# The order of weight casts and PSUM copies on ScalarE, and the places of four operand tiles, in a decoder step

## The chip, the cores and the metric

The kernel runs on one core of a Trainium2 chip. A core has TensorE (PE in the profile; PEld is its weight load), VectorE (DVE), ScalarE (ACT), GpSimd (POOL) and SyncE (SP), which here issues the DMA transfers. Each engine works through its own queue of instructions in order; semaphores tie the engines together. The metric is the device time of one execution in microseconds. Matmul operands are read from SBUF, results are summed in PSUM and must be copied or added out of it before a bank is used anew.

## The reference

One layer of a hybrid decoder runs for 1024 prompt positions and 64 sample positions (8 sequences of 8), all in float32, with a model width of 1024 and an inner width of 2816:

```
h = rmsnorm(x, norm_mix)
q, k, v, gu, gv, ga, gb = split_in(h @ w_in)
o = sink_attention(q, k, v)                      # branch A, window of 128
s = gelu(gu) * spatial_gating(layernorm(gelu(gv)))   # branch B, chunks of 128
x = x + (sigmoid(ga) * (o @ w_pa) + sigmoid(gb) * (s @ w_pb)) @ w_out
z = rmsnorm(x, norm_ffn) @ w_up                  # 1024 -> 2 * 2816
c = causal depthwise conv of width 3 over z
a, b = split(c)
x = x + (gelu(a) * b) @ w_down
y = rmsnorm(x, norm_final)
```

The outputs are y for both groups, the new key, value and convolution states and the normalised gMLP rows.

## The kernel before

Float32 products are made from matmuls in a rounded 32-bit format. `split(hi, lo, src)` (L41) makes the two parts of an operand: ScalarE casts `hi` from `src`, then VectorE subtracts to get `lo`. A product is then three matmuls, hi by hi, hi by lo, lo by hi. For weights the two parts are called `wh` and `wl`.

Two blocks of 128 weight columns are taken together as a pair, and the pair's 2 by 2 block product is done with seven products in place of eight (Winograd's form). For this the weights need four sums (`ws`, made on VectorE by `Weights.total`, L178) beside three raw blocks (`wraw`, loaded from HBM), seven units in all, each with its own cast and subtraction. The positions are cut into two groups: group 0 has half-rows of 288 columns, group 1 of 256. The left and right operands of group 0 lie in four tiles `t`, one for each quarter kk of the contraction, with the seven combinations and both parts (planes) in one tile; those of group 1 lie in `th` and `tl`. `both_planes` allocates the former, in a pool for the branch-A pairs and in another for the up pairs.

`Chain.product(j, w)` does one of the seven products for one group: four quarters by three matmuls, twelve in all (L310). Products 0, 2, 4 and 6 sum in bank `a`, and others in banks `d` and `c`, so a later product on a bank waits until the earlier state of it has been copied out. `keep` (L289 a copy, L291 a copy with a factor of −1) brings bank contents to SBUF on ScalarE as `k`; VectorE adds a bank to a kept copy (L296); L336 copies the last result out on ScalarE into `zb`.

`Weights.get(ahead, loads)` hands out the weights of the next unit and emits, at that point of the program, the load, sum, cast and subtraction of units up to `ahead` further on; the pairs ask for 3 ahead. The program's order is only a preference: a scheduler fills each engine's queue from its estimate of when things are ready. So casts may stand in ScalarE's queue far ahead of the place where they were emitted, and between copies.

The stages, in us of the profiled execution: up to 90 the v and gv projections (L528), from 90 to 460 the branch-A pairs (q, k, gu, gates; L310), from 460 to 770 attention, the gMLP, the merge and w_out (L242 and others), from 770 to 810 the operands of the FFN, from 810 to 1270 the up pairs (L310 again), and from 1270 the down projection (L1679) and the final norm.

In the up stage 22 pairs are done (f = 0 to 21, z for a and b halves in `za` and `zb`). Three of them, f = 0, 1, 2, run for group 0 alone at the start; their group-1 half follows at places 6, 13 and 21 of the list `order`. There PE does seven products of one group only ("single pair"), against fourteen in the others. After each pair, `finish(f)` does the convolution and the gate: on ScalarE a first term (L1557) and two gelu (L1608, L1611), on VectorE two terms for each half (L1558, L1559), the gate's products (L1613, L1614), and with every second pair four sums (L1621 to L1624) of what the down stage reads, which are stored to `td` in HBM.

Of the kernel before, what the change touches and what calls it, by code (L numbers as in the profile page):

```python
# [6 lines left out]
F32 = mybir.dt.float32  # L7
F32R = mybir.dt.float32r
I32 = mybir.dt.int32
AF = mybir.ActivationFunctionType  # L10
# [5 lines left out]
P = 128  # L16
# [18 lines left out]
def layer(tc, a):  # L35
    nc = tc.nc
    V, S, G, PE = nc.vector, nc.scalar, nc.gpsimd, nc.tensor

    def split(hi, lo, src, pin=False):

        for x in (S.copy(hi, src), V.tensor_sub(lo, src, hi.bitcast(F32))):  # L41
            if pin:
                tc.keep_in_program_order(x)

    def scale_split(hi, lo, src, by):
        S.activation(hi, src, AF.Copy, scale=by)
        V.scalar_tensor_tensor(lo, src, by, hi.bitcast(F32), ALU.mult, ALU.subtract)

    with ExitStack() as top:
# [22 lines left out]
        class Weights:  # L72
# [109 lines left out]
            def emit(self, upto):  # L182
                while self.emitted < min(upto, len(self.units)):
                    i, j = self.units[self.emitted]
                    _, k, dest = self.items[i]
                    if j not in ("own", "pre") and dest and not dest[0]():
                        break
                    self.load(i + 1)
                    t = self.raw[i][0] if j != "pre" else None
                    if j == "pre":  # L190
                        h, l = self.slot() if k > 4 else self.half(True)
                        for e, to in enumerate((h, l)):
                            self.last = nc.sync.dma_start(to[:, 0:k].bitcast(F32), dest[:, e])
                    elif j == "own":
                        h, l = self.half(False)
                        split(h, l, dest(t))
                    elif j == "dest":
                        h, l, hd, ld = dest[1]()
                        split(hd, ld, by256(t))
                    elif j == "full":  # L200
                        self.left = None
                        h, l = self.slot()
                        split(h[:, 0:k], l[:, 0:k], t[:, 0:k, :])
                    else:
                        h, l = self.half(j != "half")
                        src = t[:, 0:k, :]
                        if j != "half":
                            tb = self.raw[i][1]
                            src = (lambda: t[:, 0:4], lambda: self.total("s1"),
                                   lambda: self.total("s2"), lambda: self.total("s4"),  # L210
                                   lambda: self.total("s3"), lambda: t[:, 4:8],
                                   lambda: tb[:, 4:8])[j]()
                        split(h, l, src)
                    self.made[self.emitted] = (h, l)
                    self.emitted += 1
                    if self.emitted == len(self.units) or self.units[self.emitted][0] != i:
                        self.raw.pop(i)
                        self.sums = {}
# [13 lines left out]
        def by256(t):  # L232
            return t.rearrange("p (k h) c -> p k (h c)", h=2)
# [16 lines left out]
        def line(pool, n):  # L250

            pool.tile([P, n // 4], F32, name=f"gap{next(gaps)}", bufs=1)

        tx = [{}, {}]
# [4 lines left out]
        def right(stack, name, bufs=1):  # L259
            return stack.enter_context(tc.tile_pool(name=name, bufs=bufs, side="right", reuse_waits="tile"))  # L260

        def both_planes(pool, name):
            t = pool.tile([P, 7, 2, 288], F32R, name=name)
            line(pool, 64)
            return t[:, :, 0], t[:, :, 1]

        def combine(t4, b11, b12, b21, b22, eng=G):
# [9 lines left out]
        class Chain:  # L277
# [7 lines left out]

            def keep(self, name, src, by=1.0):
                t = self.keeps.tile([P, 288], F32, name="k" + name, bufs=2)[:, :self.n2]
                if by == 1.0:
                    S.copy(t, src)  # L289
                else:  # L290
                    S.activation(t, src, AF.Copy, scale=by)  # L291
                self.kept[name] = t

            def put(self, e, half, op, x, y):
# [3 lines left out]
            def product(self, j, w):  # L298
                name = ("adbadbc" if self.spread else "adadaca")[j]
                if self.spread:  # L300
                    j = SPREAD[j]
                first = name not in self.bank
                if first:
                    self.bank[name] = self.ps.tile([P, 512], F32, name="st")[:, :self.n2]
                ps = self.bank[name]
                wh, wl = w
                for kk in range(4):
                    th, tl = (x[:, (0, 1, 2, 6, 3, 5, 4)[j]] for x in self.tx[kk])
                    for i, (u, v) in enumerate(((wh, th), (wh, tl), (wl, th))):
                        PE.matmul(ps, u[:, kk, :], v, start=first and kk + i == 0,  # L310
                                  stop=kk == 3 and i == 2, skip_group_check=True)
                kept = self.kept
                if j == 0:
                    self.keep("1", ps)
                elif j == 1:
                    self.keep("5", ps)
                elif j == 2:
                    self.keep("u", ps)
                    if self.spread:
                        G.tensor_sub(kept["n"], kept["n"], kept["u"])  # L320
                        self.put(1, 1, G.tensor_sub, kept["n"], kept["5"])
                elif j == 3:
                    self.put(0, 1, V.tensor_add, kept["u"], ps)
                elif j == 4:
                    self.keep("n", ps, -1.0)
                    if not self.spread:
                        self.put(1, 1, G.tensor_sub, kept["n"], kept["5"])
                elif j == 5:
                    self.put(0, 0, V.tensor_add, kept["1"], ps)
                elif self.spread:  # L330
                    for to, lo, hi in self.places(1, 0):
                        V.scalar_tensor_tensor(to, pick(ps, to, lo, hi), -1.0, pick(kept["u"], to, lo, hi),
                                               ALU.mult, ALU.subtract)
                else:
                    for to, lo, hi in self.places(1, 0):
                        S.activation(to, pick(ps, to, lo, hi), AF.Copy, scale=-1.0)  # L336

        def pick(x, place, lo, hi):
            x = x[:, lo:hi]
            return x.rearrange("p (b t) -> p b t", t=8) if len(place.shape) == 3 else x  # L340
# [35 lines left out]
        with ExitStack() as ph1:  # L376
# [58 lines left out]
            order = [*range(FEW, 9), 0, *range(9, 15), 1, *range(15, NFF), 2]  # L435
# [203 lines left out]
            t0h, xr = right(th0, "T0h"), right(xro, "xr")  # L639
            txa = [{}, {}]  # L640
# [20 lines left out]
            def t0_job(kk):  # L661
                def go():
                    first, t4, rest = sums_of(0, kk)
                    txa[0][kk] = th, tl = both_planes(t0h, f"t{kk}")
                    split(th[:, 0], tl[:, 0], first)
                    split(th[:, 1:5], tl[:, 1:5], t4)
                    split(th[:, 5:7], tl[:, 5:7], rest)
                return go
# [317 lines left out]
            def acc2():  # L986
                return pmm.tile([P, 1024], F32, name="mm")
# [284 lines left out]
            for go in merge(0, 0, keep):  # L1272
                go()
            attention(groups[1], [x for c in range(1, KD) for x in merge(0, c, keep)])
            kvo.close()
            bo[0].close()
# [56 lines left out]
            for c in range(KD):  # L1333
                for at, go in enumerate(merge(1, c, operand(1))):
                    if at == 1:
                        t, u = held.pop(c)
# [37 lines left out]
            for c in range(KD):  # L1374
                xt = x_next(0, c)
                w, ps = W.get(), acc2()
# [9 lines left out]
            t0p = right(t0o, "T0")  # L1386
# [38 lines left out]
            def t0_split(kk):  # L1425

                def go():
                    x0, x1, t4 = hx.pop(kk)
                    tx[0][kk] = th, tl = both_planes(t0p, f"t0{kk}")
                    split(th[:, 0], tl[:, 0], x0[:, 0:288])  # L1430
                    split(th[:, 5:7], tl[:, 5:7], x1.rearrange("p (h c) -> p h c", h=2))
                    split(th[:, 1:5], tl[:, 1:5], t4)
                return go
# [3 lines left out]
            for c in range(KD):  # L1437
                xt = x_next(1, c)
                w, ps = W.get(1 if c < 7 else 4), acc2()
# [492 lines left out]
```

## Time and profile before

| | us |
|---|---|
| runs | 1510.43, 1511.06, 1516.56 |
| median | 1511.06 |
| profiled execution | 1511.13 |
| its span | 1509.4 |
| PE busy | 1493.9 |
| DVE busy | 1175.3 |
| ACT busy | 851.9 |
| POOL busy | 267.9 |

The span is the time from the first to the last recorded instruction, and the profiled execution's time is 1.7 us longer. Busy times are shares of the span in which an engine worked on at least one instruction; matmuls overlap in the pipeline, so a matmul's duration (0.28 to 0.3 us) is longer than the distance from its start to the next one's (0.11 to 0.13 us). In rows of a timeline the columns are the start, the duration, the engine, the line, the operation, the tiles written and read, the form and a count; square brackets give idle time ahead and who ended it. A row with x2 stands for two instructions that overlap.

### The profile page before, as it was taken

To read this page: it belongs to the slowest core of one execution; us is meant where nothing else is said; L and a number is where in the kernel's file an instruction comes from. 1 tells how busy PE (TensorE), PEld (TensorE's weight loads), DVE (VectorE), ACT (ScalarE), POOL (GpSimd) and SP (SyncE) were. 2 spreads that over 40 slices of the span, in tenths; PEclk is the share of its full clock that TensorE was granted. 3 is DMA by queue.
4 is the path that set the end of the run, shared out by engine and by line. 5 is a ranking of instruction groups with operands and counts; after the bars stand their busy time and mean duration, and the time that the engine had idled before them with its cause. 6 is when DMAs were issued, how large, how long until landed. Compare 5 with 4: busy or idle time off the path is not lost.

```text
span 1509.4 us, 30138 instructions
## 1 busy us (share of the span) xinstructions
PE 1493.9 (99%) x11538; PEld 1454.6 (96%) x11538; DVE 1175.3 (78%) x1892; ACT 851.9 (56%) x1778; POOL 267.9 (18%) x381
## 2 busy tenths in 40 slices
PE   9999999999999999999999999999999999999998
PEld 9999999999998989998989999999999999999998
DVE  7798877755576877979667988898899888685686
ACT  8557676654455765864453555555555556353463
POOL 0001000010030222320134422332142222000002
PEclk9999999999999999999999999999999999999999
DMA  7688446864779757438988323332232216983463
GB/s 257 220 275 273 153 164 223 254 211 143 244 234 291 217 178 233 159 130 303 334 297 289 134 107 122 116 124 108 101 133 109 102 65 236 328 288 103 113 186 126
DMA packets 134431, 289.88 MB, mean 192 GB/s; under 512 B 15760, under 2 KB 36560, under 8 KB 134288
## 3 DMA queue, kind: packets, MB, share of 16 engines
q1 hardware_dynamic: 134144, 287.96, 56.9%
q8 instruction: 90, 1.47, 0.4%
q14 instruction: 53, 0.43, 0.1%
q10 hardware_dynamic: 144, 0.01, 0.0%
HBM read 198.97 MB, written 90.92 MB: 192 GB/s over the span
## 4 chain that ended last, share of the span: by engine, by line
PE 81%; DVE 6%; ACT 4%; DMA 4%; issue 3%; POOL 1%; SPq 0%; POOLq 0%; ACTq 0%; DVEq 0%
PE st L310 43%; PE dn L1679 13%; PE mm L242 13%; PE st L528 7%; PE po L1226 2%; PE sc L1175 2%; DVE wl L41 1%; DMA stg<-sd 1%; PE pt L1202 1%; DMA v<-gvd 1%; ACT wh L41 1%; PE mx L809 1%; ACT s L1192 1%; DMA kd<-q 0%; DMA stg<-vnd 0%
## 5 line engine op out<-in xcount | busy, mean ns | idle before, releaser
L310 PE MATMUL st<-t,wh 128*128 128x288 f32 x2128 | 428.6, 294 | 3.0 <-ACT k L289 1.6
L310 PEld LDWEIGHTS st<-t,wh 128*128 128x128 f32 x2128 | 335.9, 188 | 4.0 <-ACT k L289 2.2
L310 PE MATMUL st<-t,wl 128*128 128x288 f32 x1064 | 312.5, 294 | 0.0
L310 PE MATMUL st<-th,wh 128*128 128x256 f32 x1064 | 295.5, 278 | 1.9 <-ACT k L289 1.8
L310 PE MATMUL st<-tl,wh 128*128 128x256 f32 x1064 | 294.2, 277 | 0.0
L310 PE MATMUL st<-th,wl 128*128 128x256 f32 x1064 | 293.9, 276 | 0.0
L310 PEld LDWEIGHTS st<-th,wh 128*128 128x128 f32 x1064 | 199.8, 188 | 3.3 <-ACT k L289 2.9
L310 PEld LDWEIGHTS st<-th,wl 128*128 128x128 f32 x1064 | 199.9, 188 | 0.0
L310 PEld LDWEIGHTS st<-t,wl 128*128 128x128 f32 x1064 | 199.8, 188 | 0.0
L310 PEld LDWEIGHTS st<-tl,wh 128*128 128x128 f32 x1064 | 199.7, 188 | 0.0
L1679 PE MATMUL dn<-th,wh 128*128 128x288 f32 (+1 forms) x616 | 176.9, 287 | 0.8 <-ACT zb L336 0.6
L1679 PE MATMUL dn<-tl,wh 128*128 128x288 f32 (+1 forms) x616 | 176.2, 286 | 0.0
L1679 PE MATMUL dn<-th,wl 128*128 128x288 f32 (+1 forms) x616 | 175.2, 284 | 0.2 <-DVE wl L41 0.2
L41 ACT CAST wh<-wraw 128x512 fp32r<-128x512 f32 (+2 forms) x188 | 129.5, 701 | 81.2 <-DMA wraw<-wt 34.2
L41 DVE TENSOR_TENSOR wl<-wraw,wh 128x512 fp32r<-128x512 f32 (+2 forms) x188 | 148.6, 804 | 30.3 <-ACT wh L41 28.2
L41 ACT CAST wh<-ws 128x512 fp32r<-128x512 f32 x168 | 102.6, 621 | 95.4 <-PE st L310 58.1
L41 DVE TENSOR_TENSOR wl<-ws,wh 128x512 fp32r<-128x512 f32 x168 | 119.1, 719 | 44.3 <-ACT wh L41 43.4
L1679 PEld LDWEIGHTS dn<-th,wh 128*128 128x128 f32 x616 | 115.6, 188 | 1.3 <-ACT zb L336 0.9
L1679 PEld LDWEIGHTS dn<-th,wl 128*128 128x128 f32 x616 | 115.9, 188 | 0.4 <-DVE wl L41 0.4
L1679 PEld LDWEIGHTS dn<-tl,wh 128*128 128x128 f32 x616 | 115.7, 188 | 0.0
L528 PE MATMUL st<-w2h,hh 128*128 128x256 f32 x288 | 80.5, 280 | 0.4 <-ACT rst L494 0.4
L528 PE MATMUL st<-w2l,hh 128*128 128x256 f32 x288 | 80.0, 278 | 0.0
(277 smaller groups left out, 3165.1 us busy)
## 6 DMA issues: line engine op xcount, KB each, us to landing
wraw<-wt SPq DMA_DIRECT2D x137, 512.0 KB
traw<-td SPq DMA_DIRECT2D x77, 272.0 KB
td<-za SPq DMA_DIRECT2D x22, 544.0 KB
q<-qd SPq DMA_DIRECT2D x16, 512.0 KB
upd<-hl SPq DMA_DIRECT2D x14, 512.0 KB
td<-t SPq DMA_DIRECT2D x11, 544.0 KB
wpart<-wt SPq DMA_DIRECT2D x22, 256.0 KB
qd<-q SPq DMA_DIRECT2D x8, 576.0 KB
```

Source lines behind the costliest of these rows:

```text
L41: for x in (S.copy(hi, src), V.tensor_sub(lo, src, hi.bitcast(F32))):
L242: PE.matmul(ps[:, lo:lo + c1 - c0], u[:, k, :], v[:, c0:c1], start=(k == 0 and i == 0), stop=(k == nk - 1 and i == 2))
L310: PE.matmul(ps, u[:, kk, :], v, start=first and kk + i == 0, stop=kk == 3 and i == 2, skip_group_check=True)
L528: PE.matmul(ps, u[:, lo:lo + P], v[:, k, :], start=k + i == 0, stop=k == KD - 1 and i == 2)
L809: PE.matmul(ps[:, P * i:P * i + P], vn[:, i], late["wst"][:, c, :], start=True, stop=True)
L1175: PE.matmul(ps[:, h, o0:256], q, kst[kv][:, e, k0:cur + P], start=e == 0, stop=e == 1)
L1192: S.activation(s[:, h], s[:, h], AF.Exp, bias=nm[:, h:h + 1], accum_out=dn[:, h:h + 1])
L1202: PE.transpose(pt[:, h * P:h * P + P], s[:, h, 0:P], ident)
L1226: PE.matmul(po, v[:, kv, :], t, start=e == 0, stop=last)
L1679: PE.matmul(place(m, e), u[:, m, :], v[:, lo:hi], start=new and i + k == 0 and (e == 0 or m % 2 == 0), stop=i == NU - 1 and k == 2, skip_g ...
```

## The change

Two things change. First, a list `row` and a function `in_row` are added: each instruction given to it depends, without a semaphore, on the last one given to it, so the scheduler has to keep them in the program's order on ScalarE's queue. Given to it are the casts of pair weights (and no other casts), the copies in `keep`, and the copies of the last product (L336). All other ScalarE instructions, such as the convolution, may still stand anywhere between them.

Second, `both_planes` is called with the quarter kk, and allocates all four tiles `t` at the first call, in the order 2, 0, 1, 3, with rows of 64 bytes between them (ahead of 2, 0 and 3, and behind 3; none between 0 and 1). Before, each tile was followed by 64 bytes. A tile has 7 · 2 · 288 · 4 = 16128 bytes, 63 times 256.

```diff
+    row = []
+
+    def in_row(x):
+
+        if row:
+            tc.add_manual_dep(x.ins, row[-1].ins.name,
+                              mybir.DependencyInfo(mybir.DependencyClass.NoSync, mybir.DependencyReason.DATA),
+                              reason="in_row")
+        row[:] = [x]
...
+    def split(hi, lo, src, pin=False, order=None):
+
+        for n, x in enumerate((S.copy(hi, src), V.tensor_sub(lo, src, hi.bitcast(F32)))):
             if pin:
                 tc.keep_in_program_order(x)
+            if order and n == 0:
+                order(x)
...
-                        split(h, l, src)
+                        split(h, l, src, order=in_row)
...
-        def both_planes(pool, name):
-            t = pool.tile([P, 7, 2, 288], F32R, name=name)
-            line(pool, 64)
+        planes = {}
+
+        def both_planes(pool, name, kk):
+            if kk == 0:
+                for x, gap in ((2, 64), (0, 64), (1, 0), (3, 64)):
+                    if gap:
+                        line(pool, gap)
+                    planes[x] = pool.tile([P, 7, 2, 288], F32R, name=f"{name}{x}")
+                line(pool, 64)
+            t = planes.pop(kk)
             return t[:, :, 0], t[:, :, 1]
...
-                if by == 1.0:
-                    S.copy(t, src)
-                else:
-                    S.activation(t, src, AF.Copy, scale=by)
+                in_row(S.copy(t, src) if by == 1.0 else S.activation(t, src, AF.Copy, scale=by))
...
-                        S.activation(to, pick(ps, to, lo, hi), AF.Copy, scale=-1.0)
+                        in_row(S.activation(to, pick(ps, to, lo, hi), AF.Copy, scale=-1.0))
...
-                    txa[0][kk] = th, tl = both_planes(t0h, f"t{kk}")
+                    txa[0][kk] = th, tl = both_planes(t0h, "t", kk)
...
-                    tx[0][kk] = th, tl = both_planes(t0p, f"t0{kk}")
+                    tx[0][kk] = th, tl = both_planes(t0p, "t0", kk)
```

Lines of the changed kernel lie some 16 lower: L310 becomes L326, L289 and L291 both become L307, L336 becomes L352, L41 becomes L51, L178 becomes L190, L1557 to L1559 become L1573 to L1575, L1679 becomes L1695.

More of the change, by code (lines that the diff above doesn't have):

```diff
@@ L37, in layer @@
     V, S, G, PE = nc.vector, nc.scalar, nc.gpsimd, nc.tensor
-    def split(hi, lo, src, pin=False):
-        for x in (S.copy(hi, src), V.tensor_sub(lo, src, hi.bitcast(F32))):
+    row = []
[7 more added lines that the diff above has]
+        for n, x in enumerate((S.copy(hi, src), V.tensor_sub(lo, src, hi.bitcast(F32)))):
             if pin:
                 tc.keep_in_program_order(x)
+            if order and n == 0:
+                order(x)
     def scale_split(hi, lo, src, by):
```

## The prediction

> **What bounds the kernel now.** I read the top of the page first, then the chain of waits, the costly groups, and last the stretches and single rows of the two stages that the change touches. The span, the busy times and two of the 40-slice rows:
>
> ```profile
> span 1509.4 us, 30138 instructions
> PE 1493.9 (99%) x11538; PEld 1454.6 (96%) x11538; DVE 1175.3 (78%) x1892; ACT 851.9 (56%) x1778; POOL 267.9 (18%) x381
> ...
> PE   9999999999999999999999999999999999999998
> ...
> PEclk9999999999999999999999999999999999999999
> ...
> PE 81%; DVE 6%; ACT 4%; DMA 4%; issue 3%; POOL 1%; SPq 0%; POOLq 0%; ACTq 0%; DVEq 0%
> ...
> L310 PE MATMUL st<-t,wh 128*128 128x288 f32 x2128 | 428.6, 294 | 3.0 <-ACT k L289 1.6
> ```
>
> TensorE is busy for 99% of the span at full clock and holds 81% of the chain that ended last. No work on PE is removed, so the time can fall by two things only: PE's idle time, and the distance between the starts of its matmuls. The waits of PE (us in total, times, longest) say how little idle time the ordered instructions cause:
>
> ```profile
> PE st L310 <- ACT k L289: 3.4, 4, 1.5
> PE st L310 <- ACT kn L291: 1.3, 1, 1.3
> ...
> PE dn L1679 <- ACT zb L336: 0.6, 1, 0.6
> ```
>
> That is 4.7 us in the pair products and 0.6 at the start of the down stage, 5.3 in all. It is the ceiling of what a better order on ScalarE can give. What a worse one can cost has no such ceiling, so I look at the slack. Stretches of the branch-A pairs, of the up pairs, and of 24 us around the first pair whose products run for group 1 alone ("single pair" below); columns are the length, then each engine's busy time:
>
> ```profile
> 90.00:460.00 370.00, 365.47 (x2989) 363.67 (x2988) 265.45 (x436) 217.56 (x434) 46.19 (x58) 1.00 0.66 218
> 810.00:1270.00 460.00, 459.02 (x3735) 457.86 (x3735) 399.34 (x579) 258.49 (x514) 134.77 (x192) 1.00 0.35 128
> 966.00:978.00 12.00, 12.00 (x104) 11.86 (x103) 11.41 (x15) 8.61 (x17) 2.85 (x2) 1.00 0.38 135
> 978.00:990.00 12.00, 12.00 (x101) 12.00 (x100) 12.00 (x16) 7.92 (x15) 7.34 (x8) 1.00 0.31 123
> ```
>
> In the branch-A pairs DVE is 72% busy (265.45 of 370) and 4.5 us of PE time are lost, some of it to the waits above. In the up pairs PE loses 1.0 us, DVE is 87% busy, and around a single pair it is full: 23.4 of 24 us. There only weights made ahead of use keep PE fed. ACT is at most 72% busy (8.61 of 12), so the order on it costs nothing by its own load; it costs where an ACT instruction waits and others stand behind it.
>
> **The change, part by part.** Counts of instructions stay the same on every engine. In program order, 920 of ACT's some 1540 instructions change place, 986 on DVE, 284 on SP's queue, 43 on POOL, 97 on PE. The casts move back by 3 to 13 places: each now sits between the copies where the program asks for it, three units ahead of its use, while before they ran as far ahead as buffers allowed. SP's moved loads of weights free their raw tile later by as much; over 810 to 1270 the DMA share is 0.35, so I cost them at nothing, and in R3 with the rest.
>
> *Placement.* A T tile is 16128 bytes, 63 times 256, so the one row of 64 bytes between tiles puts them 64 apart modulo 256: in the built program t0 to t3 lie at 224, 32, 96 and 160 before, and at 96, 96, 32 and 160 after. The starts of one product of group 0, twelve matmuls, three to a tile:
>
> ```profile
> 984.34 0.42 PE L310 MATMUL st<-t,wh 128*128 128x288 f32 x2
> ...
> 984.73 0.42 PE L310 MATMUL st<-t,wh 128*128 128x288 f32 x2
> ...
> 985.12 0.43 PE L310 MATMUL st<-t,wh 128*128 128x288 f32 x2
> ...
> 985.52 0.42 PE L310 MATMUL st<-t,wh 128*128 128x288 f32 x2
> ...
> 985.91 0.28 PE L310 MATMUL st<-th,wh 128*128 128x256 f32 x1
> ```
>
> The four tiles take 0.39, 0.39, 0.40 and 0.39 us here: 1.57 for twelve. Means of the same starts over all 266 such products (2128 + 1064 matmuls, 12 each) are 393.5 ns for the tile at 224, 392.5 at 32, 398.9 at 96, 393.0 at 160, together 1577.9. If a tile's own place sets its time, after gives 398.9 + 398.9 + 392.5 + 393.0 = 1583.3, +5.4 ns, times 266 = +1.4 us. If the step from one place to the next sets it (steps between 128 and 134 ns in these starts, some pairs of places not seen), I get 1576.5 to 1582.5, −0.4 to +1.2 us. Ends: four tiles at the best triple, −2.1; four at the worst, +4.7. I take +0.7, between the two readings. The Trainium skill ("TensorE: Matmul & The Clock Gate", section "Wait — 56ns, not 53.3ns?") gives a warm start-to-start of N/2.4 GHz plus about 2.5 ns, with no word of an operand's address; by it placement is worth nothing and the sum would be 0.7 lower. The rows disagree in size: for N = 288 it gives 122.5 ns, and twelve steps here are 1.57 us, 131 each; the measurement decides.
>
> *The order on ACT, place (i): third product of a single pair.* It accumulates on the first product's bank, so it waits for the copy k. Around the second single pair, ACT and PE:
>
> ```profile
> 1102.55 0.38 ACT L336 ACTIVATE zb<-st 128x256 f32<-128x256 f32 x1
> 1102.82 0.61 ACT L41 CAST wh<-wraw 128x512 fp32r<-128x512 f32 x1
> 1103.34 1.31 ACT L1557 ACTIVATE c<-zb,cw 128x1104 f32<-128x1104 f32 x1
> 1104.55 1.06 ACT L1608 ACTIVATE za<-c 128x1024 f32<-128x1024 f32 x1
> 1105.50 0.25 ACT L1611 ACTIVATE za<-c 128x64 f32<-128x64 f32 x1
> 1105.64 0.63 ACT L289 COPY k<-st 128x256 f32<-128x256 f32 x2
> ```
> ```profile
> 1102.28 0.28 PE L310 MATMUL st<-th,wh 128*128 128x256 f32 x1
> ...
> 1105.67 0.76 PE L310 MATMUL st<-th,wh 128*128 128x256 f32 x2
> ...
> 1260.02 0.38 PE L310 MATMUL st<-th,wh 128*128 128x256 f32 x1 [0.24 <-ACT k L289]
> ```
> ```profile
> 1106.06 150.23 PE st L310 x1225
> ```
>
> The single pair's first product starts at 1102.28 and the copy lets PE go on at 1106.06: 3.78 us. The pair's two products last 24 steps of 0.1137 (the mean of all group-1 steps; 30 steps from 1102.28 to 1105.67) = 2.73, so 1.05 is open. Before, ten matmuls of a following product were moved ahead and 0.27 was left (1106.06 − 1105.67 − 0.11); in the changed program's order they are behind, and the same six ACT instructions (zb, cast, c, the two gelu, k) stand in a row there. Three places, 1.0 each, against 0, 0.27 and, at the third (1260.02), 0.24 before: **+2.5**. Were the conv work not in the way, the waits of before would go, −0.5.
>
> *Place (ii): the pair after a single pair.* In the new order its copies k of the second product stand behind a cast of a sum, and the sum stands on DVE behind the conv of the single pair. First place, ACT then DVE:
>
> ```profile
> 985.12 0.65 ACT L289 COPY k<-st 128x288 f32<-128x288 f32 x2
> 985.89 0.62 ACT L41 CAST wh<-ws 128x512 fp32r<-128x512 f32 x1
> ```
> ```profile
> 978.18 0.41 DVE L296 TENSOR_TENSOR za<-k,st 128x256 f32<-128x256 f32 x1
> ...
> 980.73 1.36 DVE L1558 SCALAR_TENSOR_TENSOR c<-za,cw,c 128x1104 f32<-128x1104 f32 x1
> 982.01 0.68 DVE L41 TENSOR_TENSOR wl<-ws,wh 128x512 fp32r<-128x512 f32 x1
> 982.62 1.35 DVE L1559 SCALAR_TENSOR_TENSOR c<-za,cw,c 128x1104 f32<-128x1104 f32 x1
> 983.89 1.36 DVE L1558 SCALAR_TENSOR_TENSOR c<-zb,cw,c 128x1104 f32<-128x1104 f32 x1
> 985.17 0.68 DVE L178 TENSOR_TENSOR ws<-wraw 128x512 f32<-128x512 f32 x1
> ```
>
> Before, k came ahead of the cast (985.12 against 985.89) and nothing stalled. After: ACT's c 1.31, DVE's four c by 1.28 and three wl and ws by 0.61 (both from start to start) = 6.95, the cast 0.62, the copy 0.38: 9.26 us. From the end of the single pair's sixth product, PE has its seventh, 1.37, and three products of both groups at 1.58 + 1.37 = 2.94 each: 10.2. That would be 0.9 us of slack, but DVE reaches the conv 2.55 us late (978.18 to 980.73). Late by 9.26 + 2.55 − 10.2 = 1.6, and with some 0.1 for each of five handovers 2.1; the first product's copy, behind c of zb, adds an estimated 0.5. Lower end 0 (DVE takes the sums first), upper end 2.9. I take 2.6 at this place, 0.7 at the second, where fewer early units were missing, none at the third, after which the down stage starts: **+3.3**. If these stalls go, DVE's wl is late next.
>
> *Smaller costs.* The wl behind these casts come late in the single pairs (+0.6, two waits of some 0.3, between 0 and 1.5). The down stage's first wait, 0.6, grows by 0.3, as one more cast stands ahead of zb. In the branch-A pairs one wl stands behind DVE's evacuations, +0.5 (0 to 1).
>
> *Relief in the branch-A pairs.* The longest wait for kn comes behind two casts:
>
> ```profile
> 306.56 1.12 ACT L41 CAST wh<-ws 128x512 fp32r<-128x512 f32 x2
> ```
>
> In the new order both come after kn: 1.1 of the 1.3 goes. Of the four waits for k the longest, 1.5, stays (the cast there is replaced by another), and two of the other three, 1.9 together, lose a cast of about half a microsecond each: −1.3. Together **−2.4**.
>
> Sum: 0.7 + 2.5 + 3.3 + 0.6 + 0.3 + 0.5 − 2.4 = **+5.5 us**. The profiled execution took 1511.13 us (span 1509.4), 0.07 over the median of the runs, so 1511.1 + 5.5 = 1516.6.
>
> **The rivals.** *R1, faster:* the new order takes away stalls and makes none. For it: ACT is idle for 44% of the span, the waits it removes are in the trace, and three units are some 9 us of matmuls ahead (3 × 2.94). Against it: DVE full around the single pairs. It decides if DVE reaches the conv less than 0.4 us late (10.2 − 9.26 − 0.5) at place (ii) and ACT has done the gelu before k at (i). Time: −2.4 to −5.3, placement −0.4 to −2.1: 1503.7 to 1508.3, middle 1506. *R2, nothing PE sees:* the buffers of weights cover both the relief and the stalls; for it stands that PE loses only 1.0 us in 460 now. Time: 1511 plus placement 0 to +1.4: 1511 to 1512.5. *R3, overload carries on:* the late casts free raw tiles late, loads land late, and the stalls of (i) and (ii) come back in the following pairs, where DVE at 87% needs long to catch up. The 7.2 of costs double: 1511.1 + 14.4 − 2.4 + 0.7 = 1523.8. Against it: DMA share 0.35, and 13% free on DVE win back 2.5 us in one pair of 20.6 us.
>
> **How the numbers follow.** Forecast, 1513 to 1519.5: 0.50. R1 0.16, R2 0.14, R3 0.20 (1519.5 to 1525). Leaving out 0.2 at both ends together, the range is 1507 to 1522. A measurement here tells 0.5%, 7.6 us, from no change: below 1503.5 lies about a third of R1, 0.05; above 1518.6 R3 and a few hundredths of the forecast, 0.23; the rest is 0.72.
>
> **What would show it.** Right: waits of PE for k in the three single pairs of about 1 us, one of 2 us or more in the pair after the first; the 1.3 for kn gone; tile triples at 96 near 399 ns. Wrong: the placement if a product of group 0 takes less than 1.572 us or more than 1.59; place (ii) if PE's up stage loses under 3 us in all; the relief if PE's waits in the branch-A pairs stay above 3 us; the whole, if new waits stand where no conv runs.

## The result, and the profile after

The changed kernel takes 1528.7 us (median of six runs, 1526.0 to 1531.7) against 1511.1 before: a ratio of 1.0106, with a 95% interval of 1.0085 to 1.0128. By the medians it is 17.6 us slower, by the ratio 16.0. Forecast were 5.5 us more and a range up to 1522. The profiled execution is the shortest of the six, 1526.0, with a span of 1524.3, which is 14.9 more than the span before; the other runs lie up to 5.7 us higher, two of them with a mean granted TensorE clock of 0.995 and 0.996 in place of the 0.998 of the profiled one (3 to 5 us over such a span).

The page of the changed kernel and the waits of PE (us in total, times, longest):

```profile
span 1524.3 us, 30018 instructions
...
PE 76%; DVE 10%; DMA 5%; ACT 4%; issue 3%; POOL 1%; SPq 0%; POOLq 0%; ACTq 0%; DVEq 0%
...
L326 PE MATMUL st<-t,wh 128*128 128x288 f32 x2128 | 429.2, 295 | 5.0 <-ACT k L307 4.9
```
```profile
PE st L326 <- ACT k L307: 10.2, 10, 2.0
PE dn L1695 <- ACT zb L352: 1.7, 1, 1.7
PE pt L1132 <- DVE s L1125: 1.3, 1, 1.3
...
PE st L326 <- DVE wl L51: 1.1, 3, 0.6
```

PE holds 76% of the chain that ended last in place of 81%, and DVE 10% in place of 6%. PE's waits for copies `k` rose from 3.4 to 10.2 us, and by the page's rows the idle time ahead of the pair products' matmuls with `t` and `wh` from 3.0 to 5.0, with `th` and `wh` from 1.9 to 5.3; the wait of 1.3 for `kn` is gone, as forecast. By the first and last matmul of each stage, in us:

| stretch | before | after | difference | forecast |
|---|---|---|---|---|
| up to the first pair product | 109.9 | 110.6 | +0.7 | 0 |
| branch-A pairs | 349.0 | 352.6 | +3.6 | −1.9 |
| from there to the up pairs | 351.2 | 352.6 | +1.4 | 0 |
| up pairs | 456.3 | 464.4 | +8.1 | +6.4 |
| down projection to the end | 243.1 | 244.2 | +1.1 | +0.3 |

(The +0.7 for places is left out of the column of the forecast; it was not split by stage.) In the up pairs the forecast was nearly right, and in the branch-A pairs it had the wrong sign. The difference there is the least certain: in the other profiled kernels whose casts and copies stand as before in that stage, it took 345.2 to 349.1 us, and in those with the row bound 350.6 to 358.6. Of the +1.4 behind them, 0.8 is the wait of the first transposes for `s` (1.3 above, 0.5 before). The place that I had worked out in most detail, the pair behind the first single pair, in the changed kernel's rows of ACT, DVE and PE:

```profile
993.46 0.65 ACT L307 COPY k<-st 128x288 f32<-128x288 f32 x2
...
998.13 0.62 ACT L51 CAST wh<-ws 128x512 fp32r<-128x512 f32 x1 [2.56 <-DVE ws L190]
998.66 0.67 ACT L307 COPY k<-st 128x288 f32<-128x288 f32 x2
```
```profile
994.25 1.36 DVE L1574 SCALAR_TENSOR_TENSOR c<-zb,cw,c 128x1104 f32<-128x1104 f32 x1
...
996.14 1.36 DVE L1575 SCALAR_TENSOR_TENSOR c<-zb,cw,c 128x1104 f32<-128x1104 f32 x1
997.42 0.69 DVE L190 TENSOR_TENSOR ws<-wraw 128x512 f32<-128x512 f32 x1
```
```profile
999.10 0.40 PE L326 MATMUL st<-t,wh 128*128 128x288 f32 x1 [1.97 <-ACT k L307]
```

ACT stands idle for 2.56 us before a cast whose sum DVE reaches only behind the conv; the two copies stand behind that cast, and PE waits 1.97 us for the first of them. The copy is that of the pair's second product, whose last matmul for group 0 had started at 991.93, so the result had lain in PSUM for some 6 us.

### The profile page after: what moved, and what is told of

Its sections match the earlier page's. It is cut to its first block, busy times and chain, and to the rows that moved or that the text cites. A ratio compares the mean times of both kernels' runs of the same rounds, so it can differ in the third digit from the quotient of the medians.

```text
span 1524.3 us, 30018 instructions
## 1 busy us (share of the span) xinstructions
PE 1498.7 (98%) x11538; PEld 1454.6 (95%) x11538; DVE 1158.0 (76%) x1892; ACT 851.4 (56%) x1778; POOL 302.8 (20%) x381
## 4 chain that ended last, share of the span: by engine, by line
PE 76%; DVE 10%; DMA 5%; ACT 4%; issue 3%; POOL 1%; SPq 0%; POOLq 0%; ACTq 0%; DVEq 0%
PE st L326 38%; PE dn L1695 13%; PE mm L254 13%; PE st L544 6%; DVE wl L51 2%; PE po L1242 2%; DMA v<-gvd 2%; PE sc L1191 1%; DVE tl L51 1%; PE pt L1218 1%; DVE c L1574 1%; DVE c L1575 1%; DMA stg<-sd 1%; ACT wh L51 1%; PE mx L825 1%
## 5 line engine op out<-in xcount | busy, mean ns | idle before, releaser
L326 PE MATMUL st<-t,wh 128*128 128x288 f32 x2128 | 429.2, 295 | 5.0 <-ACT k L307 4.9
L326 PEld LDWEIGHTS st<-t,wh 128*128 128x128 f32 x2128 | 335.6, 188 | 6.9 <-ACT k L307 6.5
L326 PE MATMUL st<-t,wl 128*128 128x288 f32 x1064 | 313.2, 294 | 1.4 <-DVE wl L51 1.1
L326 PE MATMUL st<-th,wh 128*128 128x256 f32 x1064 | 296.0, 278 | 5.3 <-ACT k L307 5.3
L326 PE MATMUL st<-th,wl 128*128 128x256 f32 x1064 | 295.2, 277 | 0.3
L326 PE MATMUL st<-tl,wh 128*128 128x256 f32 x1064 | 294.8, 277 | 0.0
L326 PEld LDWEIGHTS st<-th,wh 128*128 128x128 f32 x1064 | 200.0, 188 | 6.5 <-ACT k L307 6.5
L326 PEld LDWEIGHTS st<-t,wl 128*128 128x128 f32 x1064 | 200.1, 188 | 3.6 <-DVE wl L51 3.4
L326 PEld LDWEIGHTS st<-th,wl 128*128 128x128 f32 x1064 | 199.9, 188 | 1.3 <-DVE wl L51 1.3
L326 PEld LDWEIGHTS st<-tl,wh 128*128 128x128 f32 x1064 | 199.8, 188 | 0.0
L51 DVE TENSOR_TENSOR wl<-ws,wh 128x512 fp32r<-128x512 f32 x168 | 120.6, 732 | 103.4 <-ACT wh L51 102.8
L1695 PE MATMUL dn<-th,wh 128*128 128x288 f32 (+1 forms) x616 | 177.2, 288 | 1.9 <-ACT zb L352 1.7
L1695 PE MATMUL dn<-tl,wh 128*128 128x288 f32 (+1 forms) x616 | 176.5, 287 | 0.0
L51 DVE TENSOR_TENSOR wl<-wraw,wh 128x512 fp32r<-128x512 f32 (+2 forms) x188 | 149.9, 808 | 34.7 <-ACT wh L51 33.6
L1695 PE MATMUL dn<-th,wl 128*128 128x288 f32 (+1 forms) x616 | 175.6, 285 | 0.2 <-DVE wl L51 0.2
L51 ACT CAST wh<-wraw 128x512 fp32r<-128x512 f32 (+2 forms) x188 | 128.8, 706 | 53.1 <-DMA wraw<-wt 31.7
L1695 PEld LDWEIGHTS dn<-th,wh 128*128 128x128 f32 x616 | 115.8, 188 | 2.3 <-ACT zb L352 1.9
L1695 PEld LDWEIGHTS dn<-th,wl 128*128 128x128 f32 x616 | 116.0, 188 | 0.4 <-DVE wl L51 0.4
L1695 PEld LDWEIGHTS dn<-tl,wh 128*128 128x128 f32 x616 | 115.8, 188 | 0.0
L51 ACT CAST wh<-ws 128x512 fp32r<-128x512 f32 x168 | 100.4, 619 | 25.2 <-DVE ws L190 25.0
L307 ACT ACTIVATE kn<-st 128x256 f32<-128x256 f32 (+1 forms) x76 | 30.0, 397 | 125.8 <-PE st L326 125.8
L1586 POOL COPY zb<-stc 128x18 f32<-128x18 f32 x22 | 65.6, 2983 | 108.5 <-DVE c L1575 92.4
```

What stands on the lines that cost most here:

```text
L51: for n, x in enumerate((S.copy(hi, src), V.tensor_sub(lo, src, hi.bitcast(F32)))):
L307: in_row(S.copy(t, src) if by == 1.0 else S.activation(t, src, AF.Copy, scale=by))
L326: PE.matmul(ps, u[:, kk, :], v, start=first and kk + i == 0, stop=kk == 3 and i == 2, skip_group_check=True)
L1586: G.tensor_copy(z[:, 0:90].rearrange("p (b t) -> p b t", t=10)[:, :, 0:2], stc[:, f + e * NFF])
L1695: PE.matmul(place(m, e), u[:, m, :], v[:, lo:hi], start=new and i + k == 0 and (e == 0 or m % 2 == 0), stop=i == NU - 1 and k == 2, skip_g ...
```

## The experiments

Unless a diff says otherwise, an experiment is an edit of the changed kernel. Ratios are to runs of the kernel before on the same chip. "Stage lengths" are taken as in the table above, from the profiled execution.

**The order alone, the places alone.** In the first the old `both_planes` is put back; in the second the three calls of `in_row` are taken out. All instructions stand on every engine as in the changed kernel in the first, as in the kernel before in the second.

```diff
-                for x, gap in ((2, 64), (0, 64), (1, 0), (3, 64)):
-                    if gap:
-                        line(pool, gap)
+                for x in range(4):
                     planes[x] = pool.tile([P, 7, 2, 288], F32R, name=f"{name}{x}")
-                line(pool, 64)
+                    line(pool, 64)
```

> The order of ScalarE's casts and copies is bound as in the changed kernel, the four T tiles stay at their old places. Theory O (the order costs nearly all): 15 to 18 us over the kernel before, the same stalls of TensorE as in the changed kernel (about 2 us in the pair after the first single pair, 1.1 us in each single pair, 1.9 us near 301 us), and a clean product of group 0 back at 1578 ns. Theory P (the uneven places cost it): within 3 us of the kernel before.

> The four T tiles lie at the new places, the order of all instructions on every engine is that of the kernel before. Theory O: within 1.5 us of the kernel before, a clean product of group 0 at 1576 ns against 1578, which is 0.6 us less over 266 products. Theory P: 12 us or more over the kernel before.

Measured: the order alone 1529.8 us, ratio 1.0115 (1.0097 to 1.0132), PE's waits for `k` 9.8 us. The places alone 1509.2, ratio 0.9986 (0.9974 to 0.9997), 2.1 us under the kernel before. The order costs all of it, and the new places give about 2 us. Of these 2, a product of group 0 explains 0.5 (1578 to 1576 ns, times 266); the rest is not tied to a place. This kernel is the fastest of all that were run.

**The order in one half only.** With the old places, a switch binds the row up to the up pairs, or from there on.

```diff
-        if row:
+        if not row_on[0]:
+            row.clear()
+            return
+        if row:
...
+        row_on[0] = False      # True in the other
         rest = []
         for f in range(FEW):
```

> Old places; the order is bound only up to the end of the merge, so in the branch-A pairs alone. If the profiles' split by stage holds: branch-A pairs 3.6 us longer, the stretch behind them 1.5 us longer, up pairs unchanged, together 4 to 6 us over the kernel before. By my prediction's relief of 2.4 us: 1 to 2 us under it.

> Old places; the order is bound only from the up pairs on. If the profiles' split by stage holds: up pairs 8 us longer, start of the down stage 1 us later, together 8 to 10 us over the kernel before, branch-A pairs unchanged. By my prediction: 6 to 7 us over.

Measured: the first half 1517.1, ratio 1.0038 (1.0025 to 1.0050), +5.8 us; the second 1523.3, ratio 1.0083 (1.0066 to 1.0100), +12.0. Together 17.8, as much as the order alone (18.4): the parts add up. The second lies above its expectation of 8 to 10 (its up pairs took 467.0 us). The first half does cost, so the forecast relief is refuted as a net effect; its profile has 350.6 us for the branch-A pairs, 1.6 over the kernel before and 4.1 over the second run, whose branch-A pairs are not bound (346.5).

**A longer lead; casts of sums out of the row.** Two theories for the waits: the lead of weights over their use is too short (L), or copies stand behind casts that wait for a sum on DVE (H).

```diff
-                w = W.get(3, 1)
+                w = W.get(5, 1)
```
```diff
-                        split(h, l, src, order=in_row)
+                        split(h, l, src, order=None if j in (1, 2, 3, 4) else in_row)
```

The first is done at all three calls for pairs.

> The changed kernel, with weights asked for five units ahead in place of three in the branch-A pairs and the up pairs. Theory L (short lead: the bound order makes weights too late): most of the 16 us come back, under 5 us over the kernel before. Theory H (head of line: a cast that waits for a late sum on VectorE stands in ScalarE's queue with copies behind it): a longer lead moves the same casts to other places between the copies, VectorE is as full around the single pairs; 8 us or more over the kernel before, with waits of TensorE for k still above 5 us in all.

> The changed kernel, with only the casts of raw blocks and the copies bound; the casts of VectorE's sums are left to the scheduler. Theory H: the casts that can wait for VectorE leave the row, the wait of about 2 us behind the first single pair and that of 1 us near 140 us go, under 6 us over the kernel before. Theory L: the lead of raw weights stays short, 10 us or more over.

Measured: lead 5 gives 1522.0, ratio 1.0081 (1.0064 to 1.0098); sums out of the row 1528.7, ratio 1.0118 (1.0103 to 1.0133). The totals favour H and then L, and neither holds alone. By stage, both do the same in the up pairs: 458.7 and 458.4 us against 464.4, so some 6 of the 8 us come back. Between 970 and 1006, PE waits 0.8 us for `k` with lead 5 (first row), and 3.4 in the changed kernel (second):

```profile
PE st L326 <- ACT k L307: 0.8, 2, 0.6
```
```profile
PE st L326 <- ACT k L307: 3.4, 3, 2.0
```

In the branch-A pairs lead 5 brings almost nothing (351.8 against 352.6), and freeing the casts of sums makes them longer, 358.6. Some 1.7 us of each of the two is a stretch at half the granted clock behind a long wait (see the last section). There the waits turn to the copy `ku` and to `wl`, `wh` (110 to 470, casts of sums free):

```profile
PE st L326 <- ACT k L307: 3.4, 7, 0.9
PE st L326 <- ACT ku L307: 3.0, 3, 1.8
PE st L326 <- DVE wl L51: 2.1, 4, 0.8
```

So in the up pairs the wait is made by two things together, a late sum on DVE and copies that may not pass its cast, and it is enough to take away one of them. For the branch-A pairs these two runs don't show that.

**Work taken away around the single pairs.**

```diff
-            ca = conv(f, za)
+            ca = conv(f, za, f >= FEW)      # without the two DVE terms if False; cb likewise
```
```diff
-            S.activation(gt[:, NS:T], ca[:, 80:1104], AF.Gelu_apprx_tanh)
+            if f not in (8, 14):            # the second gelu likewise
+                S.activation(gt[:, NS:T], ca[:, 80:1104], AF.Gelu_apprx_tanh)
```

> The changed kernel without VectorE's two conv terms in each half of the three single pairs (twelve instructions of 1.28 us are left out). If VectorE's full queue is what delays the sum ahead of the copies: the waits of 0.6 and 2.1 us behind the first single pair and of 0.8 us behind the second go, some 3.5 us less than the changed kernel; the waits of 1.1 us inside the single pairs stay. If ScalarE's own load or the order alone does it: the waits behind the single pairs stay within 0.3 us.

> The changed kernel without ScalarE's two gelu instructions in the pair ahead of the first and of the second single pair (1.3 us on ScalarE each are left out). By my place (i): the waits of 1.1 us at the third product of these two single pairs go, as 1.3 us are taken from a path that is 1.1 us too long, and the third single pair keeps its 1.0; some 2 us less than the changed kernel. If the copy waits for something else, they stay.

Measured, as idle steps between starts of PE (us beyond the usual distance):

| place | changed kernel | no conv terms | no gelu |
|---|---|---|---|
| third product, first single pair | 1.15 | 1.14 | 0 |
| inside it | 0.50 | 0.49 | 0.16 + 0.89 |
| pair behind it | 0.56 + 2.13 | 1.66 | 0.60 + 2.56 |
| third product, second single pair | 1.14 | 1.14 | 0 |
| inside it | 0.26 | 0.26 | 0.15 |
| pair behind it | 0.82 | 0 | 1.81 |
| third product, third single pair | 0.98 | 0.98 | 0.98 |

Without the gelu the two waits of place (i) go and the third stays, just as expected; but the pairs behind wait longer:

```profile
1001.49 0.40 PE L326 MATMUL st<-t,wh 128*128 128x288 f32 x1 [2.40 <-ACT k L307]
...
1136.45 0.41 PE L326 MATMUL st<-t,wh 128*128 128x288 f32 x1 [1.64 <-ACT k L307]
```

(In the changed kernel these are 1.97 and 0.65.) Of the 2.3 us taken away only 0.4 is won: PE comes to the next copies earlier, and DVE does not come to the sum earlier. Without the conv terms the waits behind the single pairs fall by 1.9 us, not by 3.5: at the first place the copy now stands behind the gelu, which the scheduler has moved ahead of it. For place (i) and for the pair behind the second single pair this shows the cause I gave; behind the first it shows it in part, as the queue changed with the edit. They are one backlog, whose price cannot be had place by place. The total times of these two kernels, one run each, 1531.4 and 1528.2, tell nothing against the changed kernel, as their branch-A pairs came out 2.5 and 2.0 us longer without an edit there; in the first, two stretches at half clock there make up 3.4 us.

**The row lifted around single pairs; two rows in place of one.**

```diff
+            row_on[0] = f >= FEW and (at == 0 or order[at - 1] >= FEW)
             za, zb = z_pair()
             if f < FEW:
```
```diff
-    row = []
+    rows = [[], []]
...
-    def in_row(x):
+    def in_row(x, row=rows[0]):           # copies are given to rows[1]
```

> The changed kernel, with the row lifted for the three single pairs and for the pair behind each. By my places (i) and (ii): the up stage returns from 464.4 us to 457 to 459, the first wait of the down stage and the branch-A pairs stay as in the changed kernel; 7 to 10 us over the kernel before. If the short lead over the whole up stage does it (theory L): freeing six pairs leaves casts ahead of them late, the up stage stays over 461 us, 11 us or more over.

> New places; casts are bound to the program's order among themselves, and copies among themselves, but not the ones to the others. If the tie between the two kinds is the cause: within 2 us of the kernel with the new places alone, so 0 to 4 us under the kernel before. If the order of the casts alone is: 8 us or more over the kernel before.

Measured: row lifted 1522.3, ratio 1.0062 (1.0049 to 1.0076), up pairs 460.7. Two rows 1510.7, ratio 0.9999 (0.9987 to 1.0011). The second says that the order among casts, and among copies, costs nothing here: with the two kinds untied, 1715 of ScalarE's 1778 instructions stand where they stood in the kernel before, so that kernel nearly kept both orders already. The tie between the two kinds is what costs. The first lies between its two expectations. Around the first single pair the waits are nearly gone (970 to 1006):

```profile
PE st L329 <- ACT k L310: 0.5, 1, 0.5
PE st L329 <- DVE wl L54: 0.3, 1, 0.3
```

The up pairs are still some 5 us over those of the places alone (455.6). About 3 of them sit at their start (841 to 852 us), where three pairs run for group 0 alone, a place that the prediction did not price; the rest is waits of 0.5 to 0.7 us in and behind the single pairs. The same view as in the prediction, of the kernel before, for three stretches in which PE runs one group only (first, second and fourth row) and one with both groups (third):

```profile
110.00:145.00 35.00, 35.00 (x268) 35.00 (x267) 31.00 (x53) 24.43 (x49) 6.29 (x6) 1.00 0.85 282
...
825.00:855.00 30.00, 30.00 (x234) 29.96 (x234) 29.93 (x57) 18.70 (x40) 12.02 (x15) 1.00 0.55 192
860.00:960.00 100.00, 100.00 (x818) 100.00 (x818) 82.56 (x115) 55.10 (x110) 24.50 (x40) 1.00 0.30 111
966.00:990.00 24.00, 24.00 (x203) 23.86 (x202) 23.41 (x30) 16.53 (x32) 10.19 (x9) 1.00 0.35 129
```

DVE is busy for 89, 100 and 98% in the one-group stretches, and 83% where both groups run.

**The row lifted for all one-group pairs, and for the norms too.**

```diff
+                row_on[0] = FEWA < at < len(seq) - FEWA   # branch A; second run: and at not in (9, 10, 11, 12)
                 for j in range(7):
...
+            row_on[0] = False                             # the three pairs at the start of the up stage
             za, zb = z_pair()
             ch = up_chain(0, za, zb, True)
```

> The changed kernel, with the row lifted for all pairs that run for one group only (three at the start and three at the end of the branch-A pairs, three at the start of the up stage, three single pairs in it) and for the pair behind each such stretch. If the bound order costs only where VectorE and ScalarE have a unit of weights to make for one product of PE in place of two: the waits near 140 us and near 845 us go, the up stage returns to 456 to 457.5 us, the branch-A pairs keep the wait near 302 us; 2 to 6 us over the kernel before. If the short lead elsewhere costs too: 8 us or more over.

> As the run before, and the row is lifted too for the four branch-A pairs during which ScalarE normalises the gMLP's v rows, whose instructions wait for loads. If these waits at the head of ScalarE's queue are the rest of the cost in the branch-A pairs: within 2 us of the kernel before, and within 3 us of the kernel with the new places alone. If not: as the run before.

Measured: the first 1513.1, ratio 1.0018 (1.0005 to 1.0032), with branch-A pairs of 347.3 us and up pairs of 458.1. The row still binds twelve of the thirteen two-group pairs of branch A and all but two of the nineteen of the up stage (the first of them too, which the expectation counts as free). Lifting it elsewhere took away 15 us by the medians and 13 by the ratios, and the waits near 140 and 845 us are gone. Some 4 us over the places alone are left. Its profile shows 2.5 of them in the up pairs, most of it as waits of 0.3 to 0.7 us at their start and in the single pairs, where the row is lifted, and none in the branch-A pairs (347.3 against 347.1). What binding the two-group pairs costs by itself is therefore little, but not measured apart. The second run came out slower, 1516.7, ratio 1.0037 (1.0025 to 1.0048): lifting the row during the norms costs 3.7 us. My reading that the norms' loads at the head of ScalarE's queue are the rest of the cost is refuted; in these four pairs the row rather helps, if the pairs around them are bound. I have no account of that.

**Other places.** Two alternations of the four tiles between two places, in the order of the kernel before.

```diff
-                for x, gap in ((2, 64), (0, 64), (1, 0), (3, 64)):
+                for x, gap in ((0, 64), (2, 0), (1, 128), (3, 0)):   # 32 and 160
+                for x, gap in ((0, 0), (2, 0), (1, 128), (3, 0)):    # 224 and 96, with 128 behind them
```

> The order of the kernel before; T tiles 0 and 2 at 32, 1 and 3 at 160 modulo 256, so that each matmul of group 0 reads from the other of these two places than the one ahead of it. If the step from place to place sets the distance of starts (32 to 160 to 32: 132.1 ns, 160 to 32 to 160: 128.6 to 129.6): a product of twelve takes 1564 to 1570 ns against 1578, 2 to 4 us under the kernel before. If a tile's own place sets it (392.5 at 32, 393.0 at 160): 1571 ns, 1.9 us under. If places do nothing: 1578 and the time of the kernel before.

> The order of the kernel before; T tiles 0 and 2 at 224, 1 and 3 at 96, the other alternation. By steps (224 to 96 to 224: 131.9 ns, 96 to 224 to 96: 132.4 to 133.0): a product of twelve takes 1586 to 1590 ns, 2 to 3 us over the kernel before. By own place (393.5 at 224, 398.9 at 96): 1585 ns, 1.8 us over. If places do nothing: 1578 and the time of the kernel before.

Measured: 32 and 160 give 1519.3, ratio 1.0047 (1.0032 to 1.0063), 7.5 us slower, where 2 to 4 faster was expected. 224 and 96 give 1512.4, ratio 1.0002 (0.9994 to 1.0011), no change. A product of group 0 takes 1593 ns in the first, 1584 in the second. In the 100 us from 870, without a wait of PE, the number behind PE's busy time counts the matmuls done; kernel before, places alone, 32 and 160, 224 and 96:

```profile
870.00:970.00 100.00, 100.00 (x820) 100.00 (x819) 82.22 (x117) 53.60 (x109) 24.71 (x40) 1.00 0.30 111
```
```profile
870.00:970.00 100.00, 100.00 (x822) 100.00 (x821) 82.43 (x117) 53.88 (x110) 24.82 (x40) 1.00 0.30 114
```
```profile
870.00:970.00 100.00, 100.00 (x810) 100.00 (x809) 81.41 (x116) 52.90 (x105) 23.25 (x39) 1.00 0.29 106
```
```profile
870.00:970.00 100.00, 100.00 (x819) 100.00 (x818) 81.95 (x117) 53.34 (x107) 24.60 (x40) 1.00 0.31 111
```

## Why the prediction was wrong

The direction was right, and in the up stage the mechanism too: copies behind casts that wait for a sum, where DVE is full. The size was a third of what was measured, and three of the terms failed: the places, the relief in the branch-A pairs, and the start of the down stage. The prediction's own sign that the whole is wrong, "if new waits stand where no conv runs", came true near 140 and 301 us and at the start of the up pairs.

*Placement, +0.7: wrong in sign.* Measured −2.1 (by the interval, −3.9 to −0.5), with triples at 96 near 397 ns where I had 399, and the one at 32 at 389 where I had 392.5. Both of my readings, own place and step from place to place, are refuted as rules by the alternation of 32 and 160, for which they gave 1571 and 1564 to 1570 ns, and which took 1593.

*Place (i), 1.0 at three places: right.* Measured 1.15, 1.14 and 0.98 by starts; its cause, the instructions ahead of the copy, is shown by the run without the gelu.

*Place (ii), 2.6 and 0.7: right.* Measured 0.56 + 2.13 and 0.82. What I had wrong is that (i) and (ii) are terms of a sum: taking (i) away gave most of it to (ii).

*Late wl, +0.6: right* at 0.8 in the single pairs. Not seen was the start of the up pairs, 1.2 us in the profile of the changed kernel and 3.0 in that with the singles freed. These four, 2.6 (place (i), less the 0.7 of the kernel before), 3.5, 0.8 and 1.2, add up to the 8.1 that the up pairs lost.

*Relief in the branch-A pairs, −2.4, and +0.5: wrong in sign,* +3.6 measured. The wait for `kn` did go, but in the same stretch a wait of 1.70 for `k` came; near 140 us the steps lost 2.6 where I had 0.5. The rows of the changed kernel there, ACT, DVE and PE:

```profile
138.16 0.61 ACT L728 CAST th<-stg 128x512 fp32r<-128x512 f32 x1
138.72 0.62 ACT L51 CAST wh<-ws 128x512 fp32r<-128x512 f32 x1
139.25 0.39 ACT L307 COPY k<-st 128x288 f32<-128x288 f32 x1
```
```profile
137.41 0.68 DVE L729 TENSOR_TENSOR tl<-stg,th 128x512 fp32r<-128x512 f32 x1
138.01 0.68 DVE L190 TENSOR_TENSOR ws<-ws,wraw 128x512 f32<-128x512 f32 x1
```
```profile
139.69 0.41 PE L326 MATMUL st<-t,wh 128*128 128x288 f32 x1 [0.87 <-ACT k L307]
...
301.37 0.39 PE L326 MATMUL st<-th,wh 128*128 128x256 f32 x1 [1.70 <-ACT k L307]
```

Near 140 us, sum at 138.01, cast at 138.72, copy at 139.25: place (ii) again, with the operands' `tl` in the part of the conv. ScalarE's own cast of `th` ends within 0.1 us of the sum, so VectorE and ScalarE hold the weight cast there alike. The wait at 301.37 is another case, a copy behind a normalisation of the gMLP that waits for its load:

```profile
300.03 1.03 ACT L768 ACTIVATE v<-v,mr,sd 128x768 f32<-128x768 f32 x1 [2.27 <-DMA v<-gvd]
300.97 0.35 ACT L307 COPY k<-st 128x256 f32<-128x256 f32 x1
```

No term of the prediction has such a wait. With the row lifted for the one-group pairs it is gone, though the row binds that place there too; why is not shown. The step that failed is the one in "What bounds the kernel now" that took DVE for full around the single pairs only, and took 72% for the branch-A pairs as a whole. One-group pairs also run at the start and the end of branch A and at the start of the up stage, and the same view of 110 to 145 and 825 to 855 us would have shown 89 and 100%. Lifting the row for all of them takes away 13 to 15 us, the wait at 301.37 and the longer start of the down stage among them.

*Down stage, +0.3: too small,* 1.7 of wait in place of 0.6, so +1.1. A cast of raw weights ahead of `zb` waits for its load, and a conv term behind it:

```profile
1279.61 0.62 ACT L51 CAST wh<-wraw 128x512 fp32r<-128x512 f32 x1 [0.95 <-DMA wraw<-wt]
...
1280.83 1.30 ACT L1573 ACTIVATE c<-za,cw 128x1104 f32<-128x1104 f32 x1
1282.04 0.36 ACT L352 ACTIVATE zb<-st 128x256 f32<-128x256 f32 x1
```

I had costed the moved loads at nothing because the DMA share was 0.35; here a load is on the path all the same. With the row lifted for the single pairs, no wait for `zb` is left.

*R3, overload carries on:* its time was the nearest (1523.8), but that was luck, as its mechanism is not what the trace shows: in the two-group pairs from 870 to 970 the changed order lets PE run without a gap. The cost lies in stretches I hadn't counted, not in pairs that follow. *R2* held for these two-group pairs, and not for all: one in branch A has the wait at 301.37. The last 2.7 us, between the profiled executions (+14.9) and the medians (+17.6), are not located.

## What to carry to other kernels

Binding two kinds of instruction into one order on an engine can cost much, even where each kind keeps its own order at no cost, if one of them can wait for another engine: here copies out of PSUM, which TensorE needs at once, came to stand behind casts that wait for VectorE. Price such a tie by the busy share of the engine waited for, and take that share stretch by stretch, over all stretches of the same kind, not over a stage; and ask as well which instructions in the same queue wait for loads. And where several waits come from one backlog, removing one moves it to the next; price the backlog, not the waits.

## What was not expected of the hardware

With the same instructions in the same order, the places of four tiles modulo 256 changed the distance between starts: 820 matmuls in 100 us before, 822 with the new places, 810 with tiles at 32 and 160 in turn. In that last case the products of group 1 slowed too, from 113.9 to 115.1 ns a step, though their operands had not been moved. Over the 266 products of each group that is some 4 us, and the 15 ns more for each product of group 0 are another 4: together about the 7.5 us measured. Two matmuls of each group-0 product took 139.3 ns while others with the same places ahead, of their own and behind took 131.2. So the address modulo 256 of neighbours is not what sets it alone. The Trainium skill ("TensorE: Matmul & The Clock Gate", section "Wait — 56ns, not 53.3ns?") gives one fixed cost for each warm matmul and names no address; these runs disagree by 1.2% between two placements. Which property of the address counts was not found.

A wait of TensorE can also cost more than its own length. In five of the profiled executions (the order alone, lead 5, casts of sums free, no conv terms, row lifted around single pairs) the granted clock fell to 0.5 for 3.4 us, nine times in all ahead of the last 10 us, each time within 1.6 us of the end of a wait of 1.6 to 2.7 us. Such a stretch loses 1.7 us of full clock. With lead 5, the matmul behind the wait, and the stretch (the column behind the busy times is the clock):

```profile
142.34 0.53 PE L326 MATMUL st<-t,wh 128*128 128x288 f32 x2 [2.72 <-ACT k L307]
```
```profile
143.90:147.30 3.40, 3.40 (x17) 3.40 (x16) 3.40 (x7) 3.40 (x8) 0.86 (x1) 0.50 0.82 232
```

Behind other waits as long, the 1.97 and 1.70 us of the changed kernel's profile among them, the clock stayed full, so what decides it is not shown. Part of the 2.7 us that are not located may be such stretches.
